# The first sequence's normed operand from loaded transposed rows and a spread row of scales, with 26 units of column products moved

## The chip, the core and the metric

The kernel runs on one core of one Trainium2 chip. The core has a matrix engine (PE, with weight loads shown apart as PEld), a vector engine (DVE), a scalar engine (ACT), a general engine (POOL) and a queue engine for transfers (SP). PE writes only to PSUM, which has eight banks of 128 x 512 float32. The metric is the time of one execution in microseconds on the device: the median of several runs.

## The reference, cut to what matters

One encoder layer over two sequences of 512 tokens and 1024 features each: RMS norm, one wide projection into queries, keys, values, the state-space input `u` and two gates, then windowed attention and a bidirectional state-space branch, a gated merge, an output projection and a squared-ReLU MLP. What this case touches is the beginning:

```python
def rms_norm(x, g):
    xf = x.astype(jnp.float32)
    y = xf * lax.rsqrt(jnp.mean(xf * xf, axis=-1, keepdims=True) + EPS)
    return (y * g.astype(jnp.float32)).astype(x.dtype)
...
    h = rms_norm(x, ln1)
    proj = h @ w_in
    q, k, v, u, g_att, g_ssm = jnp.split(proj, IN_SPLITS, axis=-1)
```

Each token has one scale (the inverse root of its mean square), each feature one gain. PE needs `h` transposed: features on the partitions, tokens along the row.

## The kernel before, in words

**Three products for one.** Every float32 operand of a large product is split into a rounded half `hi` and a remainder `lo`; a product is hi*hi + hi*lo + lo*hi, three matmuls. `split` does this for the weights of a column (ACT copies `c_hi`, L177, DVE subtracts `c_lo`, L178), `split_strip` for the strips.

**Strips first.** While the rows of `x` still load, the key and value projection of the first sequence begins from a second, transposed copy of the input, `x_t`, which lies in DRAM. It comes in eight strips of 128 features x 512 tokens (`xr`), each with a strip of weights (`wr`). A strip is split without the token scales, only with the gain, into `hT[1]` (a place that the second sequence needs later); `strip_products` adds 12 matmuls to four banks, the `heads`. The token scale is a factor per output row, so it is put on afterwards: `scaled_heads` (ACT, L348) reads each head with `scale=scales[t]`. Three of the four heads are the three buffers of the pool that `acc()` hands out; the fourth is the pool `ps_o`.

**Rows.** `square_rows(t)` squares 128 rows of `x` on ACT with a sum (L303), and POOL makes the inverse root (L305, L306). `scale_rows(t)` multiplies the rows by it on DVE (L309). `turn_rows(s, k)` makes strip k of sequence s's operand: four PE transposes (L314) into one bank, ACT copies it with the gain as `hi` (L316), DVE computes `lo` (L317). There are 16 such calls, eight for each sequence.

**Columns as filler.** The columns of `u` and of the gates are computed by a generator, `fillers`, in which a matmul costs two units; `pull(n)` issues n units at the place where it is called. `products` (L187) takes a bank from `acc()` and runs k = 0 to 7 with three matmuls each; the first sequence of column 0 comes first, then that of column 1, then the second sequences. `pull` calls stand between the coefficient steps, in front of the tables (`pull(140)`), in each table step (44), in each step of the recurrence (15 and 14), behind it (`pull(90)`), and in the loop over groups that follows, where what is left is spread evenly down to a remainder of 108 units. So the sum of all pulls is fixed; a unit that is moved is missing elsewhere.

**The side work on DVE.** `coefficients` is a generator of small DVE instructions (73 steps); `some(n)` issues n of them. After the loop over the second sequence's `turn_rows` the remaining ones go with `while some(4): pull(6)`. Then come the tables (DVE products, PE transposes L610, state inputs L641, lag tables L553), whose lag tables go to DRAM (L665 to L667) and back, then a recurrence of 62 steps on DVE (L716 to L719), then copies of states (L727 to L731) that PE needs in L753.

**Order.** The whole front part stands under `manual_schedule` for PE, POOL, ACT, DVE and SP: each engine's instructions have the order in which the program issues them, and an engine goes through them in that order.

Of the kernel before, what the change touches and what calls it, by code (L numbers as in the profile page):

```python
# [12 lines left out]
F32 = mybir.dt.float32  # L13
# [3 lines left out]
ALU = mybir.AluOpType  # L17
AX = mybir.AxisListType

P = 128  # L20
D = 1024
SEQ = 512
NTOK = 1024
NT = NTOK // P
# [40 lines left out]
def hybrid_layer(ctx, tc, x, x_t, w_kv, rel, onehot, w_qkv, w_ug, vectors, lam, coefs, w_glu, w_out, ln2,  # L65
# [103 lines left out]
    def split(b):  # L169
        if not phase["raw"]:  # L170
            return
        raw = phase["raw"].pop(0)
        k, n = raw.shape[1:]
        if b == 0:
            loaded.append([cpool.tile([P, 2 * k, n], F32R, tag=tag, name=tag) for tag in ("c_hi", "c_lo")])
        hi, lo = [q[:, b * k:(b + 1) * k, :] for q in loaded[-1]]
        S.copy(hi, raw)  # L177
        V.tensor_sub(lo, raw, hi.bitcast(F32))  # L178
        if b == 1:
            fetch()  # L180
# [91 lines left out]
    def pull(units):  # L272
        while units > 0:
            cost = next(filler, None)
            if cost is None:
                return
            units -= cost
            phase["units"] -= cost
# [4 lines left out]
    with tc.tile_pool(name="ssmc", bufs=1) as sc, tc.tile_pool(name="xin", bufs=1, reuse_waits="tile") as xin:  # L283
# [3 lines left out]
        lam_sb = sc.tile([P, 3, GROUPS], F32, name="lam_sb")  # L287
        pr, pi = [sc.tile([P, 9, GROUPS], F32, name=n) for n in ("pr", "pi")]
        factors = sc.tile([P, NT], F32, name="factors")
        xs, scales, turned = [], {}, {}  # L290
        for t in range(NT):
            xs.append(xin.tile([P, D], F32, tag="xt", name="xt", bufs=NT))
        rel_sb = xin.tile([N_BUCKETS + 1, N_HEADS], F32, name="rel_sb")
        oh_sb = xin.tile([N_BUCKETS + 1, LINE], F32, name="oh_sb")
        ln_sb = xin.tile([N_HEADS, LINE], F32, name="ln_sb")

        def load_rows(t):
            SP.dma_start(xs[t], x[t * P:(t + 1) * P, :])

        def square_rows(t):  # L300
            junk = xin.tile([P, D], F32, tag="rn_junk", name="rn_junk")
            ss = small.tile([P, 1], F32, tag="ss", name="ss")
            S.activation(junk, xs[t], AF.Square, scale=D ** -0.5, accum_out=ss)  # L303
            scales[t] = factors[:, t:t + 1]
            GP.tensor_scalar_add(ss, ss, EPS)  # L305
            GP.tensor_tensor(scales[t], ss, neg_half[:, 0:1], op=ALU.pow)  # L306

        def scale_rows(t):
            V.tensor_scalar_mul(xs[t], xs[t], scales[t])  # L309
# [7 lines left out]
            V.scalar_tensor_tensor(hT[s][1][:, k, :], ps, gain_1[:, k:k + 1], h.bitcast(F32),  # L317
                                   op0=ALU.mult, op1=ALU.subtract)

        strips, heads = {}, []  # L320

        def load_strip(k):
            strips[k] = [xin.tile([P, HALF], F32, tag=tag, name=tag, bufs=6) for tag in ("xr", "wr")]
            for tile_, src in zip(strips[k], (x_t, w_kv)):
                SP.dma_start(tile_, src[k])

        def split_strip(k):
            xr, wr = strips[k]
            hi, lo = [q[:, k, :] for q in hT[1]]
            wh, wl = [xin.tile([P, HALF], F32R, tag=tag, name=tag, bufs=4) for tag in ("wh", "wl")]  # L330
            strips[k] = (hi, lo), (wh, wl)
            S.activation(hi, xr, AF.Copy, scale=gain_1[:, k:k + 1])
            (S.copy if k else V.tensor_copy)(wh, wr)
            V.scalar_tensor_tensor(lo, xr, gain_1[:, k:k + 1], hi.bitcast(F32), op0=ALU.mult, op1=ALU.subtract)
            V.tensor_sub(wl, wr, wh.bitcast(F32))

        def strip_products(k):
# [3 lines left out]
            for p, t in passes:  # L341
                a, b = ((0, 0), (1, 0), (0, 1))[p]
                PE.matmul(heads[t], act[a][:, t * P:(t + 1) * P], w[b], start=k + p == 0, stop=k == KT - 1 and p == 2)

        def scaled_heads():
            for t in range(NB):
                kv = xin.tile([P, 2, N_KV, HD], F32, tag="xr", name="kv", bufs=6)
                S.activation(kv.rearrange("p a h d -> p (a h d)"), heads[t], AF.Copy, scale=scales[t])  # L348
                GP.dma_start(kv_scr[:, t], kv)

# [91 lines left out]
        def some(n):  # L442
            return len(list(itertools.islice(coefs_left, n)))
# [15 lines left out]
        square_rows(0)  # L459
        split_strip(3)  # L460
        strip_products(3)
        scale_rows(0)
        some(2)
        square_rows(1)
        split_strip(4)
        strip_products(4)
        scale_rows(1)
        square_rows(2)
        square_rows(3)
        some(4)  # L470
        scale_rows(2)
        split_strip(5)
        scale_rows(3)
        strip_products(5)
        split_strip(6)
        split_strip(7)
        split(0)
        split(1)
        some(3)
        square_rows(4)  # L480
        for k in (0, 1):
            turn_rows(0, k)
        strip_products(6)
        square_rows(5)
        scale_rows(4)
        some(5)
        for k in (2, 3, 4):
            turn_rows(0, k)
        scale_rows(5)
        square_rows(6)  # L490
        strip_products(7)
        scaled_heads()
        some(4)
        for k in (5, 6):
            turn_rows(0, k)
        scale_rows(6)
        pull(12)
        turn_rows(0, 7)
        square_rows(7)
        split(0)  # L500
        split(1)
        scale_rows(7)
        some(5)
        pull(54)
        for k in range(KT):
            turn_rows(1, k)
            pull(6)
# [27 lines left out]
    with tc.tile_pool(name="hst", bufs=1) as hp:  # L535
# [11 lines left out]
        with tc.tile_pool(name="ssmt", bufs=2) as sp:  # L547
# [121 lines left out]
                pending.insert(0, all_lags)  # L669

            pending = []
            pull(140)
            for c in range(KT):
                tables(c)
                if c == 1:
# [9 lines left out]
        with tc.tile_pool(name="ssmo", bufs=2) as sp:  # L685
# [49 lines left out]
                S.dma_start(y_scr[:, :, ga:ga + SI].rearrange("t c g k -> (t c) (g k)"), y.rearrange("p g k -> p (g k)"))  # L735

            states = [state_rows(0), state_rows(1)]
            pull(90)
            full = None
            for q in range(GROUPS // SH):  # L740
                g0 = q * SH
# [1116 lines left out]
```

## Time and profile before

| what | value |
|---|---|
| median of 3 runs | 1445.42 us (1445.25 to 1445.69) |
| the profiled execution | 1445.04 us |
| its span, first to last instruction | 1443.3 us |
| PE busy | 1435.6 us, 99% |
| PEld busy | 1228.0 us, 85% |
| DVE busy | 1094.9 us, 76% |
| ACT busy | 762.3 us, 53% |
| POOL busy | 244.1 us, 17% |

The profile is of one execution. Its lines name the line of the kernel, the engine, the operation and `out<-in`. In an order of time the first number is the start and the second the length in us, both from the span's start; a number in brackets is the idle time before, and what ended it. In the groups stand the count, the busy time, the mean of one in ns, and the idle time in front. The chain of waits goes back from the last instruction to whatever released each step. The ends of matmuls are modelled, so a PE that is called busy can overlap its neighbours; starts are the better measure.

### The profile page before, as it was taken

To read this page: it belongs to the slowest core of one execution; us is meant where nothing else is said; L and a number is where in the kernel's file an instruction comes from. 1 tells how busy PE (TensorE), PEld (TensorE's weight loads), DVE (VectorE), ACT (ScalarE), POOL (GpSimd) and SP (SyncE) were. 2 spreads that over 40 slices of the span, in tenths; PEclk is the share of its full clock that TensorE was granted. 3 is DMA by queue.
4 is the path that set the end of the run, shared out by engine and by line. 5 is a ranking of instruction groups with operands and counts; after the bars stand their busy time and mean duration, and the time that the engine had idled before them with its cause. 6 is when DMAs were issued, how large, how long until landed. Compare 5 with 4: busy or idle time off the path is not lost.

```text
span 1443.3 us, 22044 instructions
## 1 busy us (share of the span) xinstructions
PE 1435.6 (99%) x7997; PEld 1228.0 (85%) x7997; DVE 1094.9 (76%) x1978; ACT 762.3 (53%) x1359; POOL 244.1 (17%) x396
## 2 busy tenths in 40 slices
PE   9999999999999999999999999999999999999998
PEld 8888888889999999988888888888888888888887
DVE  7999959995458999988976588777776597575644
ACT  7678861224448887894444255455454443333332
POOL 3144443004244432263100000000000000000000
PEclk9999999999999999999999999999999999999999
DMA  7356549529651533345552344444442983464341
GB/s 297 97 170 189 168 147 327 206 91 314 227 180 59 162 107 100 119 140 189 194 190 91 129 136 173 161 160 155 151 143 96 363 319 102 146 201 145 121 131 59
DMA packets 102204, 240.23 MB, mean 166 GB/s; under 512 B 12330, under 2 KB 25130, under 8 KB 102096
## 3 DMA queue, kind: packets, MB, share of 16 engines
q1 hardware_dynamic: 62304, 139.94, 29.9%
q0 software_dynamic: 16320, 48.28, 10.2%
q10 hardware_dynamic: 23472, 50.61, 9.5%
q8 instruction: 63, 1.03, 0.3%
q14 instruction: 45, 0.37, 0.1%
HBM read 169.02 MB, written 81.82 MB: 174 GB/s over the span
## 4 chain that ended last, share of the span: by engine, by line
PE 84%; DVE 8%; issue 4%; DMA 2%; ACT 1%; POOL 1%; DVEq 0%; SPq 0%; ACTq 0%; POOLq 0%
PE bank L118 14%; PE bank L120 14%; PE bank L119 14%; PE acc L187 9%; PE acc L125 6%; PE acc L919 5%; PE po L1002 2%; PE sps L970 2%; PE sps L641 2%; PE tps L986 2%; PE sps L753 2%; PE acc L120 2%; PE acc L119 2%; PE acc L118 2%; DVE t L716 2%
## 5 line engine op out<-in xcount | busy, mean ns | idle before, releaser
L187 PE MATMUL acc<-act,c_hi 128*128 128x512 f32 x768 | 243.7, 395 | 0.0
L119 PE MATMUL bank<-b_lo,a_hi 128*128 128x512 f32 (+1 forms) x449 | 174.4, 389 | 0.0
L120 PE MATMUL bank<-b_hi,a_lo 128*128 128x512 f32 (+1 forms) x449 | 174.4, 389 | 0.0
L118 PE MATMUL bank<-b_hi,a_hi 128*128 128x512 f32 (+1 forms) x449 | 174.4, 389 | 0.0
L187 PEld LDWEIGHTS acc<-act,c_hi 128*128 128x128 f32 x768 | 142.3, 188 | 27.8 <-ACT act L316 0.9
L1714 ACT CAST a_hi<-d_a 128x1024 fp32r<-128x1024 f32 x56 | 59.1, 1055 | 177.4 <-PE bank L119 173.2
L187 PE MATMUL acc<-act,c_lo 128*128 128x512 f32 x384 | 151.3, 394 | 0.0
L1715 DVE TENSOR_TENSOR a_lo<-d_a,a_hi 128x1024 fp32r<-128x1024 f32 x56 | 68.5, 1223 | 98.5 <-ACT a_hi L1714 98.5
L118 PE MATMUL bank<-act,act 128*128 128x512 f32 x368 | 143.2, 389 | 0.0
L119 PE MATMUL bank<-act,act 128*128 128x512 f32 x368 | 143.2, 389 | 0.0
L120 PE MATMUL bank<-act,act 128*128 128x512 f32 x368 | 143.2, 389 | 0.0
L919 PE MATMUL acc<-w_hi,act 128*128 128x256 f32 x512 | 114.0, 291 | 0.1
L119 PEld LDWEIGHTS bank<-b_lo,a_hi 128*128 128x128 f32 x449 | 84.3, 188 | 17.5
L120 PEld LDWEIGHTS bank<-b_hi,a_lo 128*128 128x128 f32 x449 | 84.3, 188 | 17.5
L118 PEld LDWEIGHTS bank<-b_hi,a_hi 128*128 128x128 f32 x449 | 84.3, 188 | 17.3
L919 PEld LDWEIGHTS acc<-w_hi,act 128*128 128x128 f32 x512 | 87.0, 189 | 4.0 <-PE sps L970 0.3
L187 PEld LDWEIGHTS acc<-act,c_lo 128*128 128x128 f32 x384 | 72.2, 188 | 14.7 <-DVE c_lo L178 0.8
L125 PE MATMUL acc<-act,gc_hi 128*128 128x512 f32 x256 | 81.2, 394 | 0.3 <-POOL act L1066 0.3
L118 PEld LDWEIGHTS bank<-act,act 128*128 128x128 f32 x368 | 69.1, 188 | 14.4
L120 PEld LDWEIGHTS bank<-act,act 128*128 128x128 f32 x368 | 69.1, 188 | 14.3
L119 PEld LDWEIGHTS bank<-act,act 128*128 128x128 f32 x368 | 69.1, 188 | 14.2
L980 ACT ACTIVATE p<-p,nmx 128x257 f32<-128x257 f32 (+1 forms) x128 | 72.0, 563 | 16.5 <-DVE nmx L974 15.5
(365 smaller groups left out, 3424.4 us busy)
## 6 DMA issues: line engine op xcount, KB each, us to landing
d_a<-a_scr SPq DMA_DIRECT2D x56, 512.0 KB, 3.6
raws<-in_w_up_dram SPq DMA_DIRECT2D x32, 512.0 KB, 4.0
a_scr<-t ACTq DMA_DIRECT2D x64, 256.0 KB, 3.0
k<-in_w_down_dram SPq DMA_DIRECT2D x32, 512.0 KB, 5.6
c_raw<-in_w_ug_dram SPq DMA_DIRECT2D x48, 256.0 KB, 4.1
ct_scr<-ctab POOLq DMA_DIRECT2D x16, 512.0 KB, 4.8
ctab_in<-ct_scr POOLq DMA_DIRECT2D x16, 512.0 KB, 6.4
a_scr<-a ACTq DMA_DIRECT2D x32, 256.0 KB, 2.0
```

The lines of the kernel that those rows point to most:

```text
L118: PE.matmul(ps, a[0], b[0], start=first, stop=False)
L119: PE.matmul(ps, a[0], b[1], start=False, stop=False)
L120: PE.matmul(ps, a[1], b[0], start=False, stop=last)
L125: PE.matmul(ps, w[wi][:, k, :], rows[yi], start=k + p == 0, stop=k == KT - 1 and p == 2)
L187: PE.matmul(ps, w[wi][:, k, :], hT[s][hi][:, k, :], start=n == 0, stop=n == 3 * KT - 1)
L641: PE.matmul(ps[:, i * P:(i + 1) * P], bm[:, ri, g, :], u_sb[:, gp * SH + g, :], start=True, stop=True)
L716: V.tensor_mul(t1, h[:, i], a8r)
L753: PE.matmul(o, ctab[:, g0 % SI + g, ri, 0:T * CH], st[:, ri, g].rearrange("p s k -> p (s k)"), start=False, stop=ri == 1)
L919: PE.matmul(self.ps, hT[sq][act][:, k, col:col + P], w[:, k % 4, :], start=i == 0, stop=i == 3 * KT - 1)
L980: S.activation(p, p, AF.Exp, bias=self.nmx[:, h:h + 1], scale=-1.0, accum_out=self.sums[:, h, self.qb:self.qb + 1])
L1714: S.copy(hi, src)
L1715: V.tensor_sub(lo, src, hi.bitcast(F32))
```

## The change

For the first sequence, `turn_rows(0, k)` and `scale_rows(0..3)` go. Instead `spread_scales` lets POOL copy each token scale across 128 columns (`wide`) and PE transpose these four tiles into the bank `idle`: the result is one bank in which every partition holds the row of 512 token scales. `normed_strip(k)` then multiplies the strip `xr`, which stays loaded, by gain and that row on DVE (in place), copies it as `hi` on ACT, and subtracts for `lo` on DVE (even k) or POOL (odd k). To keep the strips, `xr` has eight buffers, not six; the row tiles `xt` have five, not eight, and `kv` has two of its own. The order of the calls in this part is written anew. 26 units of columns go from behind the recurrence to the front of the tables.

```diff
-            xs.append(xin.tile([P, D], F32, tag="xt", name="xt", bufs=NT))
+            xs.append(xin.tile([P, D], F32, tag="xt", name="xt", bufs=5))
...
-            strips[k] = [xin.tile([P, HALF], F32, tag=tag, name=tag, bufs=6) for tag in ("xr", "wr")]
+            strips[k] = [xin.tile([P, HALF], F32, tag=tag, name=tag, bufs=n) for tag, n in (("xr", KT), ("wr", 6))]
+            raws_t.append(strips[k][0])
...
+        def spread_scales():
+            wide = xin.tile([P, NB, P], F32, name="wide")
+            ps = idle
+            for t in range(NB):
+                GP.tensor_copy(wide[:, t], scales[t].to_broadcast([P, P]))
+                PE.transpose(ps[:, t * P:(t + 1) * P], wide[:, t], ident)
+            spread.append(ps)
+
+        def normed_strip(k, eng=V):
+            xr, (hi, lo) = raws_t[k], [q[:, k, :] for q in hT[0]]
+            V.scalar_tensor_tensor(xr, xr, gain_1[:, k:k + 1], spread[0], op0=ALU.mult, op1=ALU.mult)
+            S.copy(hi, xr)
+            eng.tensor_tensor(lo, xr, hi.bitcast(F32), op=ALU.subtract)
+
         def scaled_heads():
             for t in range(NB):
-                kv = xin.tile([P, 2, N_KV, HD], F32, tag="xr", name="kv", bufs=6)
+                kv = xin.tile([P, 2, N_KV, HD], F32, tag="kv", name="kv", bufs=2)
...
         split_strip(3)
         strip_products(3)
-        scale_rows(0)
-        some(2)
+        some(3)
         square_rows(1)
         split_strip(4)
         strip_products(4)
-        scale_rows(1)
         square_rows(2)
         square_rows(3)
-        some(4)
-        scale_rows(2)
+        some(6)
         split_strip(5)
-        scale_rows(3)
         strip_products(5)
         split_strip(6)
+        spread_scales()
         split_strip(7)
+        normed_strip(0)
+        normed_strip(1, GP)
+        strip_products(6)
+        split(0)
+        normed_strip(2)
+        normed_strip(3, GP)
+        split(1)
+        normed_strip(4)
+        normed_strip(5, GP)
+        square_rows(4)
+        normed_strip(6)
+        normed_strip(7, GP)
+        strip_products(7)
+        scaled_heads()
+        square_rows(5)
+        scale_rows(4)
+        scale_rows(5)
+        square_rows(6)
+        pull(18)
         split(0)
         split(1)
-        some(3)
-        square_rows(4)
-        for k in (0, 1):
-            turn_rows(0, k)
-        strip_products(6)
-        square_rows(5)
-        scale_rows(4)
-        some(5)
-        for k in (2, 3, 4):
-            turn_rows(0, k)
-        scale_rows(5)
-        square_rows(6)
-        strip_products(7)
-        scaled_heads()
-        some(4)
-        for k in (5, 6):
-            turn_rows(0, k)
+        some(2)
+        square_rows(7)
         scale_rows(6)
-        pull(12)
-        turn_rows(0, 7)
-        square_rows(7)
-        split(0)
-        split(1)
         scale_rows(7)
-        some(5)
-        pull(54)
+        some(8)
+        pull(48)
         for k in range(KT):
             turn_rows(1, k)
             pull(6)
...
-            pull(140)
+            pull(166)
             for c in range(KT):
                 tables(c)
...
-            pull(90)
+            pull(64)
```

More of the change, by code (lines that the diff above doesn't have):

```diff
@@ L289, in hybrid_layer @@
         factors = sc.tile([P, NT], F32, name="factors")
-        xs, scales, turned = [], {}, {}
-        for t in range(NT):
-            xs.append(xin.tile([P, D], F32, tag="xt", name="xt", bufs=NT))
+        xs, scales = [], {}
         rel_sb = xin.tile([N_BUCKETS + 1, N_HEADS], F32, name="rel_sb")
@@ L318, in turn_rows @@
                                    op0=ALU.mult, op1=ALU.subtract)
-        strips, heads = {}, []
+        strips, heads, spread, raws_t = {}, [], [], []
         def load_strip(k):
-            strips[k] = [xin.tile([P, HALF], F32, tag=tag, name=tag, bufs=6) for tag in ("xr", "wr")]
+            strips[k] = [xin.tile([P, HALF], F32, tag=tag, name=tag, bufs=n) for tag, n in (("xr", KT), ("wr", 6))]
+            raws_t.append(strips[k][0])
             for tile_, src in zip(strips[k], (x_t, w_kv)):
```

## The prediction

> **What bounds the kernel now.** I read the page first, then the waits of PE, then PE's order of time, then the chain of waits; DVE and ACT only for the places where PE meets them.
>
> ```profile
> span 1443.3 us, 22044 instructions
> ...
> PE 1435.6 (99%) x7997; PEld 1228.0 (85%) x7997; DVE 1094.9 (76%) x1978; ACT 762.3 (53%) x1359; POOL 244.1 (17%) x396
> ```
>
> PE works through 1435.6 of 1443.3 us. The time is therefore PE's work plus PE's stops, and the waits of PE say how few stops there are:
>
> ```profile
> PE sps L753 <- DVE st L731: 0.4, 1, 0.4
> ```
>
> That is the longest wait on a compute engine after the start, 0.4 us in one place. An edit can only gain by giving PE less to do, and it loses whatever PE must newly wait for. PE in order of time, at the places that the change touches:
>
> ```profile
> 22.87 0.60 PE L314 MATMUL sps<-ident,xt 128*128 128x128 f32 x4
> ...
> 39.53 0.60 PE L314 MATMUL sps<-ident,xt 128*128 128x128 f32 x4
> ...
> 67.82 1.03 PE L610 MATMUL tps<-ident,bpre 128*128 128x128 f32 x8
> 320.68 0.61 PE L753 MATMUL sps<-st,ctab_in 128*128 128x128 f32 x4
> ```
>
> At 22.87 strip 5 is done and the first turned rows begin; at 39.53 the loop over the second sequence; at 67.82 the tables; at 320.68 the first product that needs states. The chain of waits gives the prices of PE's steps:
>
> ```profile
> 28.02 2.11 PE acc L343 x9
> 49.76 18.23 PE acc L187 x79
> 73.86 1.78 PE sps L641 x16
> 209.91 1.58 DMA lag_scr<-ks
> ```
>
> A strip matmul takes 2.11/9 = 0.234 us, a column matmul 18.23/79 = 0.231.
>
> **PE's own work.** From 22.87 to 39.53 are 16.66 us. They hold strips 6 and 7 (24 matmuls), 33 column matmuls (pulls of 12 and 54 units, two units each) and eight groups of four transposes. 57 x 0.2335 = 13.31, so a group costs 3.35/8 = 0.42 us. Eight go and one comes (the spread row): **-2.9 us**. Without a stop, strip 7 would end at 22.87 + 0.42 + 24 x 0.234 = 28.9.
>
> **What column 0 now waits for.** Two things, and the second decides. First, every step k of column 0 needs both halves of strip k's normed operand. Second, `heads` holds the three banks that `acc()` hands out, so column 0's bank is free only after ACT has scaled head 0 (L348). ACT works in program order, and the changed order puts `scaled_heads()` behind all eight `normed_strip` copies, two weight splits and the squares of rows 4. Before, it stood ahead of turned rows 5 to 7:
>
> ```profile
> 23.51 0.69 ACT L316 ACTIVATE act<-sps,vec 128x512 fp32r<-128x512 f32 x1
> ...
> 29.95 1.85 ACT L348 ACTIVATE kv<-acc,factors 128x512 f32<-128x512 f32 x3
> 24.23 0.75 DVE L317 SCALAR_TENSOR_TENSOR act<-sps,vec,act 128x512 fp32r<-128x512 f32 x1 [0.29 <-ACT act L316]
> 24.90 0.74 DVE L317 SCALAR_TENSOR_TENSOR act<-tps,vec,act 128x512 fp32r<-128x512 f32 x1
> 17.66 1.11 POOL L306 TENSOR_TENSOR factors<-ss,neg_half 128x1 f32<-128x1 f32 x1
> ```
>
> The rows also give the hand-overs: ACT starts at 23.51, 0.04 after the transposes end (22.87 + 0.60), DVE 0.03 after ACT ends, and the next DVE instruction, if it waits for nobody, 0.08 before the last one ends. Prices of the steps:
>
> ```profile
> L303 ACT ACTIVATE rn_junk<-xt 128x1024 f32<-128x1024 f32 x8 | 8.6, 1071 | 2.0 <-DMA xt<-in_x_dram 1.9
> L334 DVE SCALAR_TENSOR_TENSOR act<-xr,vec,act 128x512 fp32r<-128x512 f32 x8 | 6.0, 746 | 0.2
> L178 DVE TENSOR_TENSOR c_lo<-c_raw,c_hi 128x512 fp32r<-128x512 f32 x8 | 5.3, 687 | 0.6 <-ACT c_hi L177 0.5
> L177 ACT CAST c_hi<-c_raw 128x512 fp32r<-128x512 f32 x8 | 4.9, 635 | 3.1 <-DMA c_raw<-in_w_ug_dram 3.0
> L303 ACT ACTIVATION_READ_ACCUMULATOR rn_junk<-xt 128x1 f32 x8 | 1.6, 197 | 0.0
> L348 ACT ACTIVATE kv<-acc,factors 128x512 f32<-128x512 f32 x3 | 1.9, 703 | 0.0
> L1066 POOL TENSOR_TENSOR act<-act,act 128x512 fp32r<-128x512 f32 x16 | 20.4, 1292 | 4.5 <-ACT act L1069 4.4
> L888 POOL COPY kd<-kn 128x512 f32<-128x512 f32 x8 | 4.9, 610 | 0.0
> ```
>
> The spread row: POOL has the fourth factor at 18.8. The trace has no 128x128 spread copy; four of them cost between nothing and 2.4 us (0.61 each by the row with four times the elements). Either way they are done by 21.2, and PE comes to them only at 22.87, so I take nothing. So spread is readable at 23.5. From there DVE and ACT take turns, since the new product (0.75), the copy (0.63) and DVE's own subtraction (0.69) of a strip wait for each other. The new product has one input in PSUM, as L317 has, and one in SBUF, as L334 has; both rows say 0.75.
>
> A pair of strips: product 0.75, copy 0.63, subtraction 0.69, second product 0.75, each a hand-over apart: 2.75 until the second product has ended. Then `split` follows: ACT copies the second strip and then a weight half, which ends 1.21 later, DVE subtracts it (0.69), and 4.65 us after the first start comes the next pair. Two such pairs: 23.51 + 9.30 = 32.81. The third pair has no split, but ACT squares rows 4 behind its second copy, from 36.2 to 37.3 (1.07 and 0.20, overlapped by 0.1), so strip 6's copy, whose product was ready at 36.3, runs 37.3 to 38.0; subtraction to 38.7, product 7 to 39.35, copy 7 to 40.0, head 0 scaled at **40.65**. POOL's subtraction of strip 7 (1.29) ends at 41.3, and PE needs it only 21 matmuls after 40.65.
>
> PE stands from 28.9 to 40.65: **11.75 us** that the trace of before does not have. Queued behind it are all of PE's later instructions; nothing else is offered to PE.
>
> **The restart.** After a stand PE does not start at full pace here:
>
> ```profile
> 1.07 3.78 PE L372 MATMUL tps<-running 128*128 128x128 f32 x16 [1.07 <-DVE running L369]
> 5.19 1.62 PE L343 MATMUL acc<-wh,act 128*128 128x512 f32 x3 [0.33 <-DVE wh L333]
> ...
> 7.00 0.86 PE L343 MATMUL acc<-wh,act 128*128 128x512 f32 x3
> ```
>
> Sixteen 128x128 matmuls took 3.78 us, against 1.78 for sixteen of L641; the four first strip matmuls took 1.81 (5.19 to 7.00), against 0.93 later. That is half pace for almost 6 us and 2.0 + 0.9 = 2.9 us lost. Only the start of the span shows this, so inside the kernel it costs between 0 and 2.9; I take **+2.7**, near the only row there is. The Trainium skill (TensorE: Matmul & The Clock Gate, "Why this matters for your kernels") says that a gap of over about 3 us between bursts puts the array back to half clock. By its window of 3.4 us, one to two windows at half pace, an estimate would be 1.7 to 3.4. No run shown has a gap inside the kernel, so its rule is untested; it speaks against this change.
>
> **After the stand.** From 40.65 come 33 column matmuls, 7.7 us, and 2.7 for the pace: the loop begins at 51.1 instead of 39.5, **+11.5**. (At full pace it would be 48.4, and the scaled rows 7 would hold it some 0.3 more: ACT has three heads, the squares of rows 5 and 6, two weight halves and the squares of rows 7 first, 3 x 0.63 + 3 x 1.17 + 1.2, so to 47.2; POOL's power and DVE's scaling follow.) The loop's shape stays. Then come 13 more column matmuls (26 units), and 3 more because four coefficient steps fewer are done ahead of the loop, so `while some(4)` runs a fourth time with its six units: 16 x 0.231 = **+3.7**. The tables begin 15.2 us late. DVE is no limit there:
>
> ```profile
> 40.89 0.75 DVE L317 SCALAR_TENSOR_TENSOR act<-sps,vec,act 128x512 fp32r<-128x512 f32 x1 [1.73 <-ACT act L316]
> ...
> 64.27 1.28 DVE L600 TENSOR_TENSOR bpre<-tb,bpre 128x512 f32<-128x512 f32 x2
> 212.10 0.42 DVE L716 TENSOR_TENSOR t<-h,a8r 128x256 f32<-128x256 f32 x1 [7.74 <-PE acc L187]
> ...
> 318.92 0.43 DVE L719 TENSOR_TENSOR h<-t,t 128x256 f32<-128x256 f32 x1
> ...
> 319.43 1.10 ACT L729 COPY st<-h 64x512 f32<-64x512 f32 x1 [9.04 <-DVE h L719]
> ```
>
> The first table input is ready 24.7 us after the loop's first product on DVE (40.89 to 65.55), which itself is 1.4 behind PE's start of it, and PE comes 28.3 us after that start now, 32.0 then; four coefficient steps and a split that move behind the loop fit, even at 0.75 each (1.4 + 24.7 + 3.75 = 29.8).
>
> **The 26 units taken from behind the recurrence.** DVE's recurrence starts (212.1) when the lag tables have landed (211.5), which PE's last table step sets off, and ends at 319.35; ACT's half of the first state is there at 320.53, and PE takes it at 320.68, 0.15 us later. With the tables 15.2 late, the states come 15.2 late; PE comes with 13 matmuls less and stands 3.0 us there. So the shift behind the recurrence is 15.2, whatever was saved in front. The six units taken out in front of the tables are missing from the later pulls: -0.7 where PE is the bound.
>
> **Sum:** +11.5 + 3.7 - 0.7 = **+14.5** on the profiled 1445.04 (span 1443.3 and 1.7 around it): 1459.5, and 0.4 more for the median of the runs, 1445.42: **1459.9**. As work and stops: -2.9 + 11.75 + 2.7 + 3.0 = 14.55. Anything under 0.2%, 2.9 us, could not be told from no change.
>
> **Rivals.**
> - *Full pace after the stand.* Matmul rows inside the span are steady, for want of a gap. Then 0.3 replaces 2.7: 1457.5. Chance 0.17.
> - *A second slow start.* The stand of 3.0 in front of L753 also costs pace: 2.7 more, 1462.6. The span's only other gap, 0.34 at 4.85 to 5.19, tells nothing. Chance 0.09.
> - *The bank is no limit.* If head 0 is scaled early, PE follows the strips: strip 7's low half at 41.3, two matmuls and nine more, loop at 44.0, +4.5; with 3.7 - 0.7 it is 1452.9. Every ACT row shown is in program order, against it. Chance 0.06.
> - *Faster: the strips keep up.* If DVE and ACT deliver head 0 by 28.9 and each strip before its step, PE does not stand, and if the recurrence also has slack, only the -2.9 is left: 1442.5. It needs a chain of some 17 us to take 5.4 after the spread. Chance 0.04.
> - *Same.* The strips keep up but the recurrence sets the end: the tables begin 0.8 late (3.7 - 2.9), less the 0.7: 1445.5. Chance 0.03.
>
> The forecast itself keeps 0.61, with 1457 to 1461.5 as its own range (0.3 to 3.4 for the restart, 1 us for seventeen hand-overs). The range 1452.5 to 1463 takes in the first three rivals. Slower 0.93, same 0.03, faster 0.04.
>
> **What would show it.** PE idle about 11.7 us in front of column 0's first L187, released by ACT's scaling of the heads; half pace for some 5 us behind it; tables at about 83; a 3 us wait of L753 on the state copies; DVE waiting on ACT in `normed_strip`. It is wrong if PE's idle before column 0 is under 5 us, or the loop over the second sequence starts before 45.

## The result, and the profile after

After takes 1469.69 us in the median of 5 runs (1467.95 to 1469.94), before 1445.25 (1444.52 to 1445.69): the ratio is 1.0167, 95% interval 1.0153 to 1.0182. The change makes the kernel slower by 24.4 us. The forecast was 14.5 slower, 1459.9, with a range up to 1463.0: the direction is right, the size is 9.8 too small, and the result lies outside the range. One execution of experiment e15, 1671.63 us at a granted clock of 0.81 where all others have 0.99 or more, was in a slower state of the chip and is left out of its time. The profiled execution has a span of 1468.1 us, 24.8 more than that of before.

The page of after, its first two lines of busy time:

```profile
span 1468.1 us, 21991 instructions
...
PE 1439.2 (98%) x7969; PEld 1227.4 (84%) x7969; DVE 1096.9 (75%) x1978; ACT 761.8 (52%) x1359; POOL 251.3 (17%) x404
```

PE has 28 instructions less and is busy 3.6 us longer; the other 21 us are stops. The waits of PE in after (us in total, times, longest):

```profile
PE acc L187 <- ACT kv L362: 12.6, 1, 12.6
PE sps L763 <- ACT st L739: 3.2, 1, 3.2
PE acc L187 <- DVE c_lo L178: 2.9, 4, 1.2
PE sps L651 <- DMA u_sb<-u_scr: 1.5, 1, 1.5
...
PE sps L313 <- DVE xt L308: 0.9, 1, 0.9
PE bank L119 <- DVE b_lo L1725: 0.6, 1, 0.6
```

The first row is the forecast stand in front of column 0, at its place and with its releaser; the second is the forecast stand in front of the first state product (L763 here, L753 before). The four below were in no term. PE in order of time in after:

```profile
41.33 1.22 PE L187 MATMUL acc<-act,c_hi 128*128 128x512 f32 x2 [12.60 <-ACT kv L362]
...
51.69 0.49 PE L313 MATMUL sps<-ident,xt 128*128 128x128 f32 x3
53.09 0.33 PE L313 MATMUL sps<-ident,xt 128*128 128x128 f32 x1 [0.91 <-DVE xt L308]
...
84.94 1.03 PE L620 MATMUL tps<-ident,bpre 128*128 128x128 f32 x8
...
343.79 1.02 PE L763 MATMUL sps<-st,ctab_in 128*128 128x128 f32 x4 [3.23 <-ACT st L739]
```

The first two matmuls behind the stand take 1.22 and the first state products 1.02, where before showed 0.61 for the latter. The table by stretches of after says why; behind the five pairs of busy time and count of PE, PEld, DVE, ACT and POOL stand the granted clock, the DMA share and the GB/s:

```profile
28.00:32.00 4.00, 0.73 (x4) 0.24 (x2) 2.53 (x4) 1.37 (x3) 0.06 (x1) 1.00 0.21 66
32.00:36.00 4.00, 0.00 (x0) 0.00 (x0) 2.90 (x4) 1.00 (x2) 1.21 (x1) 0.68 0.18 66
...
42.00:44.00 2.00, 2.00 (x6) 1.57 (x5) 0.00 (x0) 0.00 (x0) 1.19 (x3) 0.50 0.35 131
...
46.00:48.00 2.00, 2.00 (x8) 1.53 (x8) 0.00 (x0) 1.97 (x4) 1.36 (x4) 0.73 0.41 154
48.00:50.00 2.00, 2.00 (x10) 1.55 (x9) 1.52 (x3) 2.00 (x5) 1.62 (x3) 1.00 0.30 113
...
344.00:346.00 2.00, 2.00 (x11) 2.00 (x11) 1.59 (x3) 1.60 (x3) 0.00 (x0) 0.51 0.24 94
346.00:348.00 2.00, 2.00 (x9) 1.63 (x9) 0.00 (x0) 1.97 (x4) 0.00 (x0) 0.64 0.42 168
```

PE runs at half clock from 41.3 to about 47 (the clock itself had fallen at 33.4, while PE stood) and again from 344 to about 347.4: both stands were followed by a slow start, the second of which was only a rival. The shift against before at the places that order the work, from the timelines of both profiled executions:

| place | before | after | shift | forecast |
|---|---|---|---|---|
| loop over the second sequence | 39.53 | 51.69 | +12.2 | +11.5 |
| first table | 67.82 | 84.94 | +17.1 | +15.2 |
| last lag table on PE | 200.19 | 218.84 | +18.7 | +15.2 |
| recurrence starts on DVE | 212.10 | 233.36 | +21.3 | +15.2 |
| recurrence's last step | 318.92 | 342.18 | +23.3 | +15.2 |
| last state product | 394.57 | 417.81 | +23.2 | +15.2 less part of 0.7 |
| end of the span | 1443.3 | 1468.1 | +24.8 | +14.5 |

### The profile page after: what moved, and what is told of

It reads as the page before. It is cut to its first block, busy times and chain, and to the rows that moved or that the text cites. A ratio compares the mean times of both kernels' runs of the same rounds, so it can differ in the third digit from the quotient of the medians.

```text
span 1468.1 us, 21991 instructions
## 1 busy us (share of the span) xinstructions
PE 1439.2 (98%) x7969; PEld 1227.4 (84%) x7969; DVE 1096.9 (75%) x1978; ACT 761.8 (52%) x1359; POOL 251.3 (17%) x404
## 4 chain that ended last, share of the span: by engine, by line
PE 81%; DVE 9%; issue 4%; DMA 3%; ACT 2%; POOL 1%; DVEq 0%; SPq 0%; ACTq 0%; POOLq 0%
PE bank L119 13%; PE bank L120 13%; PE bank L118 13%; PE acc L187 9%; PE acc L125 6%; PE acc L929 6%; PE po L1012 2%; PE sps L980 2%; PE tps L996 2%; PE sps L763 2%; PE sps L651 2%; PE acc L119 2%; PE acc L120 2%; PE acc L118 2%; DVE t L726 1%
## 5 line engine op out<-in xcount | busy, mean ns | idle before, releaser
L187 PE MATMUL acc<-act,c_hi 128*128 128x512 f32 x768 | 246.1, 398 | 12.6 <-ACT kv L362 12.6
L119 PEld LDWEIGHTS bank<-act,act 128*128 128x128 f32 x368 | 69.1, 188 | 14.5
L118 PEld LDWEIGHTS bank<-act,act 128*128 128x128 f32 x368 | 69.1, 188 | 14.2
```

Source lines behind the costliest of these rows:

```text
L118: PE.matmul(ps, a[0], b[0], start=first, stop=False)
L119: PE.matmul(ps, a[0], b[1], start=False, stop=False)
L187: PE.matmul(ps, w[wi][:, k, :], hT[s][hi][:, k, :], start=n == 0, stop=n == 3 * KT - 1)
```

## Experiments

Each time is a median beside runs of before on the same chip (1444.81 to 1445.06). "Units" are the pulls of column matmuls, two per matmul. My theory (A) after the result: the forecast's terms stand, and the rest is what the 26 moved units do between the tables and the end of the recurrence. The rivals: the extra waits come from the late tables as such (B), the units are neutral (C), or ACT's wait for a kv buffer lies on PE's path (e3).

**e1, the units put back in after.**

```
-            pull(166)
+            pull(140)
...
-            pull(64)
+            pull(90)
```

> The changed kernel (1469.7 us) with the 26 units put back behind the recurrence (pulls of 140 and 90). Theory A, the moved units cost in all the places behind the loop: the tables begin 3.0 us earlier; the stand of 3.2 us before L763 and the half pace behind it (1.9) go; and the three waits that the forecast did not have go too, because they come from the columns' weight loads falling at other points of the tables and the recurrence: u_sb 1.5, the late landing of the lag tables 2.6, c_lo 2.0 to 2.9. Sum about -11: 1459. Theory B, these three waits come from the late start of the tables as such: only -3.0 and -1.9 are left, 1464.8. Theory C, the units are neutral: 1469.7.

Measured 1465.49, ratio 1.0138 (1.0123 to 1.0153): 4.2 less than after, where A said some 11. Up to the last state product A held: the shift is 13.5 at the first table, 14.1 where the recurrence starts and 14.2 at its end (17.1, 21.3 and 23.3 in after), the stand behind it is gone, and at the last state product 13.0 are left in place of 23.2. Then the shift grows to 20.4, most of it in two places whose waits, in e1, are new:

```profile
PE bank L118 <- ACT act L1450: 2.1, 1, 2.1
PE acc L118 <- ACT act L1331: 1.1, 1, 1.1
```

In this order they end at 860.05 and 763.88; behind the one at 763.88 the clock is 0.66 from 765 to 770. Why ACT is late there only when the work comes 10 us sooner was not found. So e1 shows what the units cost up to 418 us, and not what they cost in the whole.

**e2, the units moved in before, nothing else.** The edit is that of e1 the other way round, in before.

> The kernel before (1445.3 us) with only the 26 units moved (pulls of 166 and 64). Theory A: the tables begin 3.0 us late, PE stands about 3 us before the first state product, half pace costs 1.9 behind it, and the waits on u_sb, lag tables and c_lo appear: up to +11, 1456. Theory B: +3.0 and +1.9, no new waits in tables and recurrence, 1450. Theory C: 1445.3.

Measured 1451.85, ratio 1.0044 (1.0027 to 1.0061): +7.0. The forecast had given these units 3.0 before the tables, repaid as a stand later. The shift is 2.0 at the tables (this profiled execution comes to column 0 1.0 earlier than that of before), 3.6 at the last lag table, 4.75 at the recurrence, 5.4 at its end, 7.35 at the last state product. The waits of PE in e2:

```profile
PE sps L753 <- ACT st L729: 3.3, 1, 3.3
PE sps L641 <- DMA u_sb<-u_scr: 1.7, 2, 0.9
...
PE acc L187 <- DVE c_lo L178: 0.8, 2, 0.5
```

The time lies between A's upper end and B. The forecast, as work and stops, had 3.0 for these units: 4.0 of the missing 9.8 are here, in a kernel that has neither the new operand nor the stand in front of column 0.

**e3, four kv buffers in place of two in after.** `name="kv", bufs=2` becomes `bufs=4`.

> The changed kernel with four buffers for kv, so that ACT no longer waits 3.1 us for the first kv transfer to land. Theory A (PE is held by the first scaled head, by its half pace and only at the very end by rows 7): the first head is scaled at the same time, only the 0.9 us wait of the loop's first turned rows goes: 1468.8. Rival (ACT's 3.1 us are on PE's path): 1466.6.

Measured 1467.42, ratio 1.0153 (1.0135 to 1.0172). The wait of 0.9 on scaled rows is gone; the waits on u_sb grow from 1.5 to 2.7. The time lies between the two expectations, and e3's four runs spread over 5.8 us and overlap those of after: inconclusive on the time. It serves as the base of e4 and e5.

**e4, PE kept busy in the stand.** To e3 are added 54 matmuls of the identity with itself behind strip 7; nobody reads their result.

```
         strip_products(7)
+        busy = sps()
+        for _ in range(54):
+            PE.matmul(busy[:, 0:P], ident, ident, start=True, stop=True)
         scaled_heads()
```

> As with four kv buffers, and PE runs 54 idle matmuls of 128x128 (their result is read by nobody) between strip 7 and column 0, some 12 us. Theory A (the pace after the stand is half because PE stood): the granted clock stays 1.00, the 13 slow matmuls of column 0 take 0.23 instead of 0.43 each, 2.6 us less, of which rows 7 leave most: 1466 to 1466.6. Rival (the pace is slow for another reason, operands arriving or the bank): 1468.8 as without them.

Measured 1461.49, ratio 1.0113 (1.0098 to 1.0128), 5.9 below e3. The stretch in which after and e3 had half clock, in e4:

```profile
42.00:44.00 2.00, 2.00 (x10) 1.64 (x10) 0.00 (x0) 1.97 (x4) 2.00 (x4) 1.00 0.35 131
```

Ten matmul records in 2 us in place of six: the slow start is shown by removing it and nothing else. Column 0 begins at 41.25, as in after, the loop at 48.87 in place of 51.06 (e3). That is 2.2; the other 3.7 came later: from the last lag table to the recurrence pass 12.6 in place of 14.5, and the rest lies scattered. A had the pace and the loop right, and the time, 1466 to 1466.6, too high.

**e5 and e6, the bank freed sooner.** e5 moves strip 7's products ahead and scales head 0 behind the fourth normed strip (on e3); e6 leaves after's order and gives all eight subtractions to POOL.

```
         strip_products(6)
+        strip_products(7)
         split(0)
         normed_strip(2)
         normed_strip(3, GP)
+        scaled_heads((0,))
...
-        strip_products(7)
-        scaled_heads()
+        scaled_heads((1, 2, 3))
```

> The changed kernel with four kv buffers, strip 7's products moved up behind strip 6's, and the first head alone scaled on ACT behind normed strip 3 instead of behind normed strip 7. Theory A (the head's bank alone holds column 0): column 0 begins at about 32.6 instead of 41.3, follows the strips and ends by 44; but rows 7 are scaled only at about 50.5, since ACT's order still has the squares of rows 5 to 7 behind the strips, so the loop begins at about 50.6 and the time falls by 2 to 3 us, to about 1467. Rival (the bank is the only limit in front of the loop): loop at 45.5, 1462. Second rival (the strips, not the bank, hold column 0): column 0 still begins after 38, 1468.8.

e6, on after:

```
-            eng.tensor_tensor(lo, xr, hi.bitcast(F32), op=ALU.subtract)
+            GP.tensor_tensor(lo, xr, hi.bitcast(F32), op=ALU.subtract)
```

> The changed kernel with all eight subtractions of the normed strips on POOL. Theory A (DVE and ACT wait for each other strip by strip, and that chain sets the first head): DVE's products no longer wait for ACT's copies, the chain from the spread row to the first scaled head shrinks from 17.5 us to about 10 (eight copies, two weight halves, one square on ACT), column 0 begins near 34 and then waits for POOL's subtractions, eight of 1.27 us, the last at about 37. The stand in front of column 0 falls to about 5 us, but rows 7 still hold the loop: 4 to 7 us gained, 1463 to 1466. Rival (POOL, at 1.3 us each and slowing DVE's two-input work, becomes the bound): no gain, 1469 to 1472.

Measured 1465.98 (ratio 1.0144, 1.0130 to 1.0158) and 1464.22 (1.0135, 1.0121 to 1.0149). Column 0 begins at 32.64 and 34.06, so it was the order on ACT, and DVE's chain in front of it, that held the bank. But the loop begins only at 49.39 and 48.22: a later thing takes the place of the first at once. In e5 it isn't the scaled rows 7, as A had it: they are ready at 49.05, and PE does not wait for them. It is the weight halves of column 1, which ACT copies behind the heads and the squares; a wait of PE in e5, with 2.6 in e6:

```profile
PE acc L187 <- ACT c_hi L177: 2.4, 1, 2.4
```

From 44.17 in e5 and 45.08 in e6 the clock is at half once more.

**e7, the same computation in another order.** normed_strip is divided into product (DVE and ACT) and remainder (the subtraction); both weight halves are split first, strips 6 and 7 run together, the heads are scaled one by one between the strips, kv has four buffers, four more coefficient steps lie ahead, and the units are where before had them.

```
+        split(0)
+        split(1)
+        square_rows(4)
+        product(0)
+        product(1)
+        square_rows(5)
+        remainder(0)
+        product(2)
+        remainder(1, GP)
...
+        scaled_heads((0,))
```

> The same computation as the changed kernel in an order that is meant to let PE run through, with the 26 units left behind the recurrence: strips 6 and 7 follow the spread row at once, column 0's weights are split while DVE waits for it, products run one strip ahead of their remainders, the first head is scaled behind the fourth copy, the squares of rows 4 to 6 stand between the strips, and kv has four buffers. Theory A (the 28 transposes less are worth 2.9 us of PE as soon as nothing stands): loop at about 36.5, no stand over 0.5 us, states met as before: 1442.4. Rival (DVE or the recurrence sets the time of the tables anyway): 1445.3 within 1. Second rival (the spread row cannot keep PE fed): over 1447.

Measured 1447.24, ratio 1.0015 (1.0006 to 1.0024). No stand at the bank (column 0 at 28.71), and with the units back 22 of the 24 us are gone. A's 1442.4 is wrong: the loop begins at 38.70, not 36.5, and the 2.9 of PE's work bring nothing. The groups on DVE in e7, from 22 to 40 us:

```profile
L360 DVE TENSOR_TENSOR act<-xr,act 128x512 fp32r<-128x512 f32 x4 | 4.9, 1224 | 0.4 <-ACT act L356 0.3
L308 DVE TENSOR_SCALAR xt<-xt,factors 128x1024 f32<-128x1024 f32 x4 | 4.1, 1040 | 0.0
```

**e8, e7 with the units moved.** The edit is that of e2: 140 and 90 become 166 and 64.

> The new order with the 26 units ahead of the tables, as the change has them. Theory A (the units are a loss of their own: tables 3.0 later, a stand of 3 before the first state product, half pace behind it): 4 to 11 us more than without them, 1446.5 to 1453. Rival (the units fill what the transposes leave free): equal to the new order without them, within 1.

Measured 1453.83, ratio 1.0068 (1.0055 to 1.0080): 6.6 over e7. With e2 this is the second base on which the units alone cost about 7. The parts are not the same: 2.0 of the cost arise only behind the last state product, and in the profiled execution no slow start follows the stand. A wait of PE in e8:

```profile
PE sps L776 <- ACT st L752: 3.4, 1, 3.4
```

The stretches of e8, in the middle of that stand and behind it:

```profile
326.00:328.00 2.00, 0.26 (x2) 0.28 (x3) 1.97 (x4) 1.38 (x2) 0.00 (x0) 1.00 0.36 129
328.00:330.00 2.00, 2.00 (x15) 1.82 (x15) 1.84 (x3) 1.98 (x4) 0.00 (x0) 1.00 0.36 130
```

**e9, e7 without POOL in it.** Four calls change:

```
-        remainder(1, GP)
+        remainder(1)
```

> The new order of e7 with all eight subtractions of the normed strips on DVE, none on POOL. A, POOL's subtractions stretch DVE's beside them and that held the loop at 38.7: each subtraction takes 0.69 again (1.19 and 2.32 in e7), each scaling of rows 0.7 (1.2 in e7), PE's waits of 0.9 on POOL and 0.6 on the weight halves go, the loop over the second sequence begins at 37 to 38, the tables no later than 67.5, and the time is 1444 to 1445.5. Rival, DVE simply has more work than before (four subtractions of 0.69 in place of POOL's, 2.8 us): the loop stays at 38.5 to 39.5, the tables at 68 to 69, and the time is 1447 to 1448.5.

Measured 1445.27, ratio 1.0004 (0.9995 to 1.0013), 2.0 below e7 by the medians; seven of its eleven runs lie between 1444.7 and 1445.5, four between 1446.7 and 1447.0, and what parts them is open. The same groups in e9:

```profile
L360 DVE TENSOR_TENSOR act<-xr,act 128x512 fp32r<-128x512 f32 x8 | 5.5, 684 | 0.1
L308 DVE TENSOR_SCALAR xt<-xt,factors 128x1024 f32<-128x1024 f32 x4 | 2.9, 750 | 0.1
```

Twice as many subtractions take DVE 0.6 us more: POOL's four had cost DVE 2.2 on its own four and 1.2 on the scalings. The loop begins at 37.26 and the tables at 66.53, 1.3 earlier than in before. Yet the end is 0.4 later: of the 1.05 still in hand at the last state product, nearly all is gone between 740 and 753 us, where PE waits 0.24 for DVE and the rest shows as no wait, and 0.3 more goes at about 1190. The change's 2.9 is thus had only in part at its place, and nothing of it at the end.

**e10, PE kept busy in front of the first state product.** e2 with 14 more matmuls; nobody reads their result.

```
             pull(64)
+            busy = sps()
+            for _ in range(14):
+                PE.matmul(busy[:, 0:P], ident, ident, start=True, stop=True)
```

> Before with the 26 units moved (e2), and 14 idle 128x128 matmuls, 0.23 us each or 3.2 in all, where PE stands in front of the first state product; nobody reads their result. A, the 3.3 us stand also cost a slow restart: the clock is 1.00 in the 8 us behind it, the last state product comes 1.9 earlier than in e2, and the time is 1449.9. Rival, the shift from 5.5 to 7.35 behind that point in e2 is something else (late inputs of the state products): the clock may be full but the time stays at 1451.8.

Measured 1451.51, ratio 1.0042 (1.0030 to 1.0055), beside 1451.85 in e2. The stretch behind the stand, e2 first, then e10:

```profile
326.00:328.00 2.00, 1.82 (x8) 1.85 (x9) 1.95 (x4) 1.98 (x4) 0.00 (x0) 0.50 0.42 131
```

```profile
326.00:328.00 2.00, 1.77 (x14) 1.56 (x14) 1.96 (x4) 2.00 (x4) 0.00 (x0) 1.00 0.43 139
```

The slow start is there in e2 and gone in e10, and the last state product comes 2.4 earlier; but 0.7 of this is given back behind it, and the medians differ by 0.3 with runs that spread over 2.4 and 2.7. In the trace A is right; on the time the run is inconclusive.

**e11, e9 with 1.3 us of DVE's work on ACT.** The squares of rows 7 also come ahead of head 1.

```
-        scale_rows(4)
+        square_rows(7)
         scaled_heads((1,))
+        scale_rows(4, True)
...
-        ... (pi, bi_p, (V.tensor_copy,) * 2)):
+        ... (pi, bi_p, (V.tensor_copy, S.copy))):
```

`True` has ACT scale the rows.

> e9 with 1.3 us of DVE's work ahead of the tables given to ACT (the scaling of rows 4 and one copy of the powers), and the squares of rows 7 ahead of the second head. A, DVE sets when the tables begin: they begin about 1 us earlier than in e9, and the time is 1 us below it, 1443 to 1444.5, which beats before. Rival, ACT is as full as DVE there (13 us of work between 24 and 38): what DVE saves, ACT's later copies give back, and the time equals that of e9 within 0.5.

Measured 1447.06, ratio 1.0015 (1.0006 to 1.0023): 1.8 above e9. ACT's weight halves come late (PE stands 1.70 in front of 36.50), as the rival said, and more: the stretches of e11 (PE alone, then the clock, the DMA share and the GB/s),

```profile
36.50:37.00 0.50, 0.50 (x2) 1.00 0.92 360
...
37.50:38.00 0.50, 0.50 (x3) 0.96 0.00 0
38.00:38.50 0.50, 0.50 (x2) 0.50 0.39 111
...
41.00:41.50 0.50, 0.50 (x3) 0.63 0.70 283
41.50:42.00 0.50, 0.50 (x5) 1.00 0.21 82
```

show the clock halved 1.5 us after PE had resumed, for 3.4 us.

**e12, e2 with the column weights split later.** From the third column on:

```
-            if splits and n in (3, 9):
-                split(n // 6)
+            if splits and n in ((3, 9) if i == 1 else (16, 22)):
+                split(int(n > 8) if i == 1 else int(n > 16))
```

> Before with the 26 units moved (e2), but the weight halves of the next column are split, and so the loads behind them issued, 13 matmuls later in each column (steps 16 and 22 in place of 3 and 9, from the third column on), which is where they stood in time before the move. A, part of what e2 lost beyond the later tables is the column loads falling on the lag tables and on the recurrence: from the last lag store to the recurrence 11.9 again (13.05 in e2), the recurrence 106.8 (107.4), no waits of PE on weight halves in it, and the time is about 2 us under e2, 1449 to 1450; the stand of 3 us before the first state product and its restart stay. Rival, the loads' place does not matter: 1451.8 as e2.

Measured 1448.80, ratio 1.0028 (1.0018 to 1.0038): 3.0 below e2. The recurrence has its 106.8 again (107.4 in e2, 108.8 in after, 106.8 in before), u_sb's waits fall from 1.7 to 0.5, and PE spends its 2.8 of spare time on weight halves before the recurrence ends, so that the stand in front of the first state product and its slow start are gone; PE in e12:

```profile
323.69 0.38 PE L750 MATMUL sps<-u_sb,toep 128*128 128x128 f32 x2
323.91 0.61 PE L753 MATMUL sps<-st,ctab_in 128*128 128x128 f32 x4
```

One thing did not go as A said: from the last lag table to the recurrence it is still 12.9, not 11.9. So the column loads were not what delays the lag tables.

**e13, e16 and e17, the gate store in front of the lag tables.** What is left in the traces is the store of a finished gate column (0.5 MB, from ACT's queue). In e2, the last store of the lag tables on POOL, the gate store on ACT, and the first step of the recurrence on DVE:

```profile
213.50 0.50 POOL L667 DMA_DIRECT2D lag_scr<-ks  x1
```

```profile
213.06 0.33 ACTq L211 DMA_DIRECT2D ga_scr<-sg  x1
```

```profile
216.85 0.42 DVE L716 TENSOR_TENSOR t<-h,a8r 128x256 f32<-128x256 f32 x1 [8.90 <-DMA lag_scr<-ks]
```

In before the gate store goes out at 212.39, after the last lag store (209.91), and the recurrence starts 2.2 behind that; in after it is at 227.40 against 228.56, and the recurrence starts 4.8 behind. e13 issues the gate stores 12 matmuls into the next column; e16 (on e2) and e17 (on after) take one store, the third gate column's, to POOL:

```
-                S.dma_start((ga_scr if kind == "a" else gs_scr)[...], dst)
+                (GP if (kind, blk) == ("a", GA_BLK + 2) else S).dma_start((ga_scr if kind == "a" else gs_scr)[...], dst)
```

> Before with the 26 units moved (e2), and the store of each finished gate column (0.5 MB) issued 12 matmuls into the next column instead of right behind the column. In the four traces where that store comes after the last store of the lag tables, the recurrence starts 2.2 us after the issue of that last store; in the six where it comes 0.4 to 1.2 us ahead of it, 2.8 to 5.1. A, the gate store in front of them delays the lag tables: the gate store goes out at about 216, the recurrence starts 2.2 behind the last lag issue again (3.35 in e2), and the time is 1.1 us below e2, 1450.7. Rival, the coincidence means nothing: 3.3 stays.

> Before with the 26 units moved (e2), and one gate store alone, that of the third gate column, issued from POOL, where it stands in program order behind the last stores of the lag tables (from ACT, in e2, it goes out at 213.06, 0.44 ahead of the last of them at 213.50). A, that store in front of them delays the lag tables: the recurrence starts 2.2 us behind the last lag issue (3.35 in e2), all else as in e2, about 1 us less. Rival, it is not that transfer: 3.3 stays.

> After, with the same one store issued from POOL. A: the recurrence starts 2.2 us behind the last lag issue in place of 4.8, and the shift from the last lag table to the recurrence falls by 2.6, to 11.9; the time is 1467 to 1468 if nothing else takes the gain. Rival, 4.8 stays, and the time with it.

e13 (1451.37, ratio 1.0045, 1.0033 to 1.0058) tests nothing: the store still went out at 213.41, since ACT's order is not written out in that stage, and 3.3 stayed. e16: 1450.70, ratio 1.0035 (1.0023 to 1.0047). POOL and DVE in e16:

```profile
212.60 0.50 POOL L667 DMA_DIRECT2D lag_scr<-ks  x1
213.10 0.58 POOL L211 DMA_DIRECT2D ga_scr<-sg  x1
```

```profile
214.89 0.42 DVE L716 TENSOR_TENSOR t<-h,a8r 128x256 f32<-128x256 f32 x1 [7.84 <-DMA lag_scr<-ks]
```

The recurrence starts 2.3 behind the last lag store in place of 3.35, by A's 1.1: shown for e2. e17: 1467.63, ratio 1.0159 (1.0145 to 1.0173), 2.1 below after; its profiled execution, the longest of its four runs (1470.47), has the recurrence 3.8 behind the last lag store, in place of 4.8. In after the gate store was therefore about 1.0 of the 2.6; what the other 1.6 is stays open. In e4 and e15 the store leads by the same 1.2, and the recurrence starts only 2.8 behind.

**e14 and e15, the late splits in after, and all together.** e14 is after with the edit of e12. e15 is e4 with that edit and that of e13.

> After, with the weight halves of the next column split 13 matmuls later (the edit that took 3.05 us off e2 in e12), nothing else. A, a part of after's excess over the forecast is the place of the column loads and splits: the waits on weight halves in the recurrence and the 3.2 us stand in front of the first state product go or shrink, the last state product comes 2 to 4 us earlier than in after, and the time is 1466 to 1467.5. Rival, with the tables 17 us late the loads fall elsewhere and the edit does nothing: 1469.5.

> After with all that the runs found besides the stand itself: kv in four buffers, 54 idle 128x128 matmuls in the stand (nobody reads their result), the late splits of e12 and the late gate stores of e13. What is left should be the stand in front of column 0 less the work saved and the 16 matmuls ahead of the tables: -2.9 + 12.6 + 3.7 = 13.4. A: 1458 to 1459, 3 under e4. Rival, the column loads are no part of it behind a 14 us shift: 1461.5 as e4.

e14: 1468.19, ratio 1.0161 (1.0148 to 1.0175), 1.5 below after, between the two. The recurrence is 106.9 long again and the stand on the states is gone; PE's spare time has become one stand of 3.2 on weight halves at 242.33, inside the recurrence, where it delays nothing. But u_sb's waits rise from 1.5 to 2.9. e15: 1460.66, ratio 1.0113 (1.0097 to 1.0128), 0.8 below e4, with runs that overlap e4's: A's 1458 to 1459 is missed by 1.7. Its shift is 14.4 at the tables, 16.2 at the last lag table (u_sb 1.9), 17.0 at the end of the recurrence, 15.9 at the end of the span. Neither slow start is left. Against the 13.4 of the stand and the moved matmuls 2.5 remain: 1.0 ahead of the tables, 1.9 on u_sb and 0.7 at the lag tables, less 1.1 behind the recurrence. The terms add up, but the late splits do not free u_sb here, as they did in e12.

## Why the prediction was right or wrong

**PE's own work, -2.9: right as far as it reaches.** Strip 7 ends at 41.33 - 12.60 = 28.73, forecast 28.9. That it is worth something at the end is another matter: in e9 it isn't.

**The stand, 11.75: right, 12.6 measured.** Head 0 is scaled when forecast said, 0.6 late, released by ACT as forecast; e5 and e6 show the order on ACT and DVE's chain to be the cause. The chain's prices held (product 0.74, subtraction 0.69) but for one. DVE in after, then POOL:

```profile
27.16 1.36 DVE L178 TENSOR_TENSOR c_lo<-c_raw,c_hi 128x512 fp32r<-128x512 f32 x1 [1.21 <-ACT c_hi L177]
...
32.42 1.33 DVE L178 TENSOR_TENSOR c_lo<-c_raw,c_hi 128x512 fp32r<-128x512 f32 x1 [1.21 <-ACT c_hi L177]
```

```profile
26.69 1.29 POOL L357 TENSOR_TENSOR act<-xr,act 128x512 fp32r<-128x512 f32 x1 [5.67 <-ACT act L356]
31.94 1.26 POOL L357 TENSOR_TENSOR act<-xr,act 128x512 fp32r<-128x512 f32 x1 [3.96 <-ACT act L356]
```

Both subtractions of weight halves, forecast at 0.69, ran beside POOL's and took twice as long: 1.3 in all.

**The slow restart, +2.7: right.** Column 0's 33 matmuls take 51.69 - 41.33 = 10.4, against 7.7 at full pace: 2.7. e4 shows it by keeping PE busy.

**The tables, +15.2: 1.9 too small.** 0.7 came from the loop's start, 0.3 is unassigned. 0.9 is the wait on the scaling of rows 7, since `kv` has two buffers, the third head waits for a store, and the squares of rows 5 to 7 stand behind it on ACT; with four buffers (e3) that wait is gone. ACT in after, then DVE's scaling of rows 7:

```profile
40.60 1.26 ACT L362 ACTIVATE kv<-acc,factors 128x512 f32<-128x512 f32 x2
44.96 0.69 ACT L362 ACTIVATE kv<-acc,factors 128x512 f32<-128x512 f32 x1 [3.10 <-DMA kv_scr<-kv]
```

```profile
52.28 0.76 DVE L308 TENSOR_SCALAR xt<-xt,factors 128x1024 f32<-128x1024 f32 x1 [0.72 <-POOL factors L305]
```

Those 3.10 were in no step; the forecast took three heads back to back.

**The step that failed** is "With the tables 15.2 late, the states come 15.2 late; PE comes with 13 matmuls less and stands 3.0 us there. So the shift behind the recurrence is 15.2, whatever was saved in front." It treats everything from the first table to the end of the recurrence as one rigid piece. The stand came (3.2), but the piece isn't rigid: it grew by 6.1, from +17.1 to +23.3. 1.5 of this is a wait on u_sb, 2.6 the later landing of the lag tables, 2.0 a longer recurrence. Thirteen matmuls more ahead of the tables shift each column's weight splits, loads and gate store by 3 us against tables and recurrence, which have no slack. Shown: the units cost 7.0 and 6.6 on two bases (e2, e8); with the units put back in after, the piece grows by 0.7 in place of 6.1 (e1); the recurrence's part goes with the place of the splits (e12, e14, e15), the landing's part with the gate store (e16 all of it, e17 a part). Not shown: what in after makes the rest of the landing late, and what exactly delays u_sb.

**The second slow start, a rival at 0.09, happened:** the clock of 0.51 at 344. From the first state product to the last pass 74.4 in after, against 72.65 in e1, e14 and e15, which have no slow start there: it cost 1.7 (in e2 2.7, beside e10). It did not replace the forecast, as the rival had it, but came on top.

**Behind that, -0.7: hidden.** Without the slow start the same stretch is 1.6 shorter than the 74.2 of before (e1, e14, e15), more than forecast; in after the slow start takes this back, and the shift stays at +23.3 to +23.2. After 418 us it grows by 1.6 more, 1.1 of it near 1205 us, where PE waits 0.6 for b_lo; e1 and e9 lose time behind the state products too, most of it between 740 and 860. Not settled.

The surplus over the forecast is 1.9 + 1.5 + 2.6 + 2.0 + 0.7 + 1.6 = 10.3, which is 24.8 - 14.5; the 0.7 in it is the forecast gain that the second slow start took back. The range erred in the same way: it took its upper end from one more restart, and allowed the moved units no cost beyond their own 3.0.

## What to carry to other kernels

Work that fills PE's gaps is not free to move: it carries splits, loads and stores with it, so look up what each of them lies beside at the new place, above all where a chain without slack (a recurrence, a landing transfer) is under way. Before replacing PE's work by work of DVE and ACT, write down the order in which the in-order engine behind it frees PE's bank; here the order (with kv in four buffers) was 16 of 24 us, from after to e8. And an operation given to POOL can cost DVE time as well: four subtractions cost it 3.4 us here (e7 beside e9).

## What the runs showed of the hardware

- *The granted clock changes at fixed steps of 3.41 us, and falls behind a step in which PE was idle for about half of it.* In after it changes at 33.43, 47.09, 344.05 and 347.46, which lie 4, 87 and 1 times 3.413 us apart, and it does so in whole steps in every trace. If each trace is cut at these steps (with PE's ends as modelled), the clock fell behind steps with 1.57 (e1) to 3.41 us of idle time, and stayed full behind steps with up to 1.74 (e8); between these two figures it went either way. So a stand of 1.70 inside one step halved it (e11), while one of 3.36, cut by a step into 1.61 and 1.74, left it at 1.00 (e8). It fell 2.1 to 4.7 us after PE had stopped, in after's second stand and in e11 when PE was at work again, and the half clock behind a stand cost 1.7 (after's second) to 2.7 us (after's first, e2). The Trainium skill (TensorE: Matmul & The Clock Gate, "Why this matters for your kernels") puts the limit at gaps of over about 3 us. The long stands agree; the 1.70 of e11 and the 3.36 of e8 do not.
- *POOL's two-input subtraction doubles DVE's.* Beside it DVE's subtraction took 1.19 to 2.32 us in place of 0.69 and the scaling of rows 1.2 in place of 0.75; the product that reads one input from PSUM kept its 0.74. The Trainium skill (Trainium Architecture — The Big Picture, "What this means for kernel authors") says that DVE and GpSimd share a pair of SBUF ports by an exclusive lock; the rows agree with it.
- *A 0.5 MB store issued 0.4 to 1.4 us ahead of the last of many small ones goes with their late landing.* Where it goes out later (before, e1, e7, e9 and e11) the recurrence starts 2.2 behind the last lag store, where it goes out ahead 2.8 to 5.1. Moving that one store took 3.35 to 2.3 in e16 and 4.8 to 3.8 in e17; so about 1 us is shown to be its doing, and the rest is not.
